# Between two stages: modulated rows by transposing back, residual rows made later, no elementwise work on POOL, accumulators summed by transfer

## The chip, the cores and the metric

The kernel runs on one NeuronCore of a Trainium2 chip. The metric is the device time of one execution in microseconds. The engines are PE (matrix multiply), DVE (VectorE), ACT (ScalarE), POOL (GpSimd) and SP, which here only issues transfers. Transfers issued by POOL are written out by software on that engine. PE reads SBUF and writes PSUM; DVE and ACT read both; POOL reads SBUF alone.

## What is computed

A trunk of two layers over 256 context rows and 512 latent rows of 1024 channels. Layer 0 mixes by a gated linear recurrence (called lru below), layer 1 by a delta-rule recurrence (rwkv). Each mixer is followed by a mixture of 64 experts, of which each row takes 8, and a shared expert. What lies between the stages is this:

```python
def _layer_norm(h, g, b):
    mu = jnp.mean(h, -1, keepdims=True); var = jnp.mean(jnp.square(h - mu), -1, keepdims=True)
    return (h - mu) * lax.rsqrt(var + LN_EPS) * g + b

def _modulate(h, shift, scale):
    return h * (1.0 + scale) + shift

for i in range(2):                       # m[0..5] are rows made from c by ada_w, for ctx and lat apart
    y = mixer_i(_modulate(h, m[0], m[1]))
    h = _layer_norm(ALPHA * h + m[2] * y, post_ln_g[i, 0], post_ln_b[i, 0])
    u = _modulate(h, m[3], m[4])
    y = moe_i(u)                         # router, 8 of 64 experts, shared expert
    h = _layer_norm(ALPHA * h + m[5] * y, post_ln_g[i, 1], post_ln_b[i, 1])
```

Layer 1 needs the latent rows alone behind its mixer, so there are six tiles of 128 rows in layer 0 and four in layer 1.

## The kernel before

The program runs eight stages in order: the lru mixer; the first output stage (rows out of the mixer, norm, modulation, routing); the first expert stage; the first transition (norm behind the experts, rows turned to channels for the next mixer); the rwkv mixer with its projections at the start; the second output stage; the second expert stage; and the end (norm behind the experts, rows out). Except for the loop over the experts, which is laid out by hand, a scheduler orders the instructions of each engine at build time from a simulation; on the chip each engine takes its own list in order, and semaphores hold it where something is not there yet.

**Output stages.** `outputs` (line 423) runs over the row tiles. For tile t it issues the product of the mixer's output with its last weights (`gemm`, two PSUM buffers of two banks) and steps a generator `res` (line 1934) that does the rest in pieces split by `yield`: load the old rows `hin`; norm (`post_ln`, line 395, in layer 0; in layer 1 the product holds all of it and `norm`, line 409, is called alone); turn the normed tile to channels by eight PE transposes into the PSUM tile `rt_px` (one buffer), evict it by eight ACT instructions with a scale and bias per channel to `rt_uT` (L1960), which holds the modulated rows as channels; make the same modulated rows in row form by two POOL instructions (L1961, L1962) for the store to `u_d`, from which the experts gather; make the residual rows, gain and bias applied, by two more (L1964, L1965) and store them to `hm_d`; then `route` (line 677). `post_ln` and `norm` run on DVE: mean and variance by `bn_stats` (L414), then an inverse square root in some dozen instructions on 128 single numbers (L314 to L326), and one ACT instruction that normalises (L421). `prepare` loads the rows of gains, biases and modulation, spread over 128 partitions (`mb`), and combines them on POOL and DVE (L1915 to L1918). Between the pieces, `Early` feeds in parts of the shared expert, whose weights are split into a high and a low part by ACT and by DVE or POOL (`ew`, L305 and L308). The routing of the last tile ends with `Mt`, which the sort of the experts waits for (L790).

**Behind the experts.** The experts add their rows into two accumulators in DRAM, turn about. `start` (line 1997) loads a tile of each, `tile_` (line 2005) adds the two on DVE (L2007), scales by m[5] on POOL (L405, in `post_ln`), adds the old rows on DVE (L406), norms, applies the gain on POOL (L2010) and the bias on DVE (L2011), and stores. In the first transition the six tiles go on into `rwkv` (line 1059), where each is turned to channels by eight PE transposes and evicted with scale and bias `mT` by ACT (L1136) and DVE (L1133) in turn, into `u`. The stored rows `h1_d` are read again at the second output stage.

Of the kernel before, what the change touches and what calls it, by code (L numbers as in the profile page):

```python
# [9 lines left out]
F32 = mybir.dt.float32  # L10
# [9 lines left out]
D = 1024  # L20
# [251 lines left out]
class Kern:  # L272
# [122 lines left out]
    def post_ln(self, wk, h, y, m2b, zn, z):  # L395
# [8 lines left out]
        else:  # L404
            nc.gpsimd.tensor_tensor(z, y, m2b, op=OP.mult)  # L405
# [17 lines left out]
    def outputs(self, n, gemm, res, early=None, last=None, read=None):  # L423
# [5 lines left out]
        for t in range(n + 1):  # L429
            if t < n:  # L430
# [3 lines left out]
                if t == n - 1 and early:  # L434
                    last()
                    early.begin()
                    feed()
            go(t - 1)
# [6 lines left out]
            go(t - 1)  # L445
            feed()
        if early:
            early.drain()
# [610 lines left out]
    def rwkv(self, first, done, prepare, res):  # L1059
# [5 lines left out]
        with ExitStack() as st:  # L1065
# [14 lines left out]
            for n, ap in (("mu", ins["rwkv_mu"][0].rearrange("c (k p) -> (c k) p", p=128)),  # L1080
# [4 lines left out]
                          ("rk", ins["rwkv_r_k"][0].rearrange("(k t) e -> k (t e)", t=2))):  # L1085
# [13 lines left out]
            with ExitStack() as s1:  # L1099
# [7 lines left out]


                zr = b1.tile([48, D], F32, name="zr")
                nc.gpsimd.memset(zr, 0.0)  # L1110
                nc.scalar.activation(indT.rearrange("h j p -> h (j p)"), zr, AF.Copy)
                nc.scalar.activation(rn, zr[:, :NTOK], AF.Copy)
# [13 lines left out]
                for t in range(NT):  # L1126
# [112 lines left out]
                for j in range(KD):  # L1239
# [4 lines left out]
                    nc.sync.dma_start(r_d[j * 128:(j + 1) * 128, :], kf[:, :NLAT])  # L1244

# [634 lines left out]
def trunk(tc, ins, out):  # L1880
# [3 lines left out]
    with ExitStack() as st:  # L1884
# [5 lines left out]
        h1_d = dp.tile([NTOK, D], F32, name="h1_d")  # L1890
        u_d = [dp.tile([n + 128, D], F32, name=f"u_d{i}") for i, n in enumerate((NTOK, NLAT))]
# [8 lines left out]
        def mixer_res(i):  # L1900
            P = {}

            def prepare(pool, psr):
                lg, lb = K.ln_params(pool, i, 0)
                P["ln"] = lg, lb
                S = (CTX, LAT) if i == 0 else (LAT,)
                for q, s in [(q, s) for s in S for q in (2, 3, 4)]:
                    P[q, s] = pool.tile([128, D], F32, name=f"mb{q}{s}")
                    if (q, s) != (2, LAT):
                        K.bcast_row(P[q, s], i, s, q)  # L1910
# [196 lines left out]
```

## Time and profile before

| | us |
|---|---|
| median of 3 runs | 3386.93 |
| lowest, highest | 3377.25, 3399.31 |
| the profiled execution | 3388.3 |
| its span, first to last instruction | 3386.4 |

The profile follows one execution. It has the busy time of each engine, the span in 40 slices, the instructions grouped by line with their mean duration and the idle time before them, the instructions in order of time, and the busy time of each engine in chosen stretches together with the clock granted to PE (1.00 is 2.4 GHz, 0.50 is 1.2 GHz). A duration on DVE or POOL holds also the time in which the instruction was held up once it had begun.

### The profile page before, as it was taken

The numbers are of one execution on the slowest core, as the hardware profiler recorded it, in microseconds if no ns is written. First come the engines' busy times: TensorE is split into PE (matmuls) and PEld (weight loads), VectorE is DVE, ScalarE is ACT, GpSimd is POOL, SyncE is SP. The second block draws the span as 40 slices with busy tenths as digits, with TensorE's granted clock in tenths as the row PEclk, the third lists the DMA queues.
The fourth block names the chain that finished last, engine by engine and source line by source line (L and its number), as shares of the span: only waits on it lengthen the run. The fifth ranks groups of instructions, "written<-read, shape, count | busy, mean of one in ns | idle before, by whom it ended". The sixth has DMA issues, their size and how long they took to land. (4 is left out here: it accounts for less than half of the span.)

```text
span 3386.4 us, 52288 instructions
## 1 busy us (share of the span) xinstructions
PE 2934.2 (87%) x17769; PEld 2051.6 (61%) x17769; DVE 2470.1 (73%) x4665; ACT 1967.2 (58%) x3771; POOL 1274.7 (38%) x1401
## 2 busy tenths in 40 slices
PE   7998758899999998298989899998976898899993
PEld 3665746666676664276757677676655665555551
DVE  3555878788878886867774677675466888789886
ACT  2765236677766776466655455553432766677772
POOL 0323543334334432422444445453453233334333
PEclk8998879999999999599985766678788999999996
DMA  6446349999999998333675765667545999999994
GB/s 219 120 138 197 136 182 273 300 330 330 336 296 319 329 319 283 130 92 118 148 192 145 190 178 143 180 176 194 159 151 185 327 316 332 326 355 352 347 337 152
DMA packets 331073, 789.94 MB, mean 233 GB/s; under 512 B 129320, under 2 KB 194136, under 8 KB 281264
## 3 DMA queue, kind: packets, MB, share of 16 engines
q1 hardware_dynamic: 278848, 676.74, 60.6%
q0 software_dynamic: 51952, 109.78, 13.4%
q8 instruction: 145, 2.38, 0.3%
q14 instruction: 128, 1.05, 0.1%
HBM read 649.90 MB, written 134.82 MB: 232 GB/s over the span
## 5 line engine op out<-in xcount | busy, mean ns | idle before, releaser
L95 PE MATMUL ph<-w1s,xs 128*128 128x512 f32 (+21 forms) x3216 | 806.4, 400 | 5.7 <-ACT xs L305 3.9
L1031 POOL DMA_INDIRECT acc_d<-yt,ix x150 | 316.7, 2112 | 933.6 <-ACT yt L141 338.9
L308 DVE TENSOR_TENSOR w1s<-w,w1s 128x1024 fp32r<-128x1024 f32 x516 | 609.2, 1222 | 63.6 <-ACT w1s L305 62.8
L95 PEld LDWEIGHTS ph<-w1s,xs 128*128 128x128 f32 (+21 forms) x3216 | 489.9, 156 | 246.5 <-DVE xs L308 10.8
L305 ACT ACTIVATE w1s<-w 128x1024 fp32r<-128x1024 f32 x516 | 516.9, 1057 | 3.9 <-DMA w<-in_moe_w_gu_dram 3.3
L95 PE MATMUL py<-w2s,hT 128*128 128x512 f32 (+22 forms) x1608 | 429.5, 416 | 50.4 <-DVE yt L138 30.3
L95 PEld LDWEIGHTS py<-w2s,hT 128*128 128x128 f32 (+22 forms) x1608 | 250.2, 163 | 174.7 <-issue 36.8
L305 ACT ACTIVATE xs<-px 128x512 fp32r<-128x512 f32 (+23 forms) x287 | 131.0, 456 | 361.0 <-DVE xs L308 238.5
L308 DVE TENSOR_TENSOR w2s<-w,w2s 128x1024 fp32r<-128x1024 f32 x258 | 303.7, 1218 | 16.2 <-ACT w2s L305 15.9
L305 ACT ACTIVATE w2s<-w 128x1024 fp32r<-128x1024 f32 x258 | 258.4, 1053 | 23.4 <-DMA w<-in_moe_w_down_dram 23.3
L308 DVE TENSOR_TENSOR xs<-px,xs 128x512 fp32r<-128x512 f32 (+23 forms) x287 | 146.4, 510 | 149.7 <-ACT xs L305 146.6
L929 POOL DMA_INDIRECT xg<-u_d,ix x150 | 209.0, 1393 | 86.0 <-issue 39.8
L141 ACT ACTIVATE yt<-py 128x512 f32<-128x512 f32 (+20 forms) x282 | 151.5, 593 | 45.5 <-PE py L95 30.0
L73 PE MATMUL px<-ident,xg 128*128 128x128 f32 (+25 forms) x1224 | 129.3, 249 | 30.6 <-DMA xg<-u_d,ix 30.6
L1680 POOL TENSOR_TENSOR SU<-SU,pC 64x128 f32<-64x128 f32 x176 | 86.3, 495 | 167.9 <-DVE SU L1700 140.8
L539 PE MATMUL in_ps<-uT,w_in 128*128 128x256 f32 (+1 forms) x768 | 144.2, 346 | 4.3 <-ACT w_in L305 2.3
L73 PEld LDWEIGHTS px<-ident,xg 128*128 128x128 f32 (+25 forms) x1224 | 110.8, 144 | 53.4 <-issue 45.1
L539 PEld LDWEIGHTS in_ps<-uT,w_in 128*128 128x128 f32 x768 | 119.5, 191 | 35.3 <-ACT w_in L305 7.4
L1179 PE MATMUL pt_ps<-xm,rw 128*128 128x256 f32 (+1 forms) x600 | 130.0, 372 | 11.9 <-ACT xm L305 6.5
L1525 PE MATMUL sc_ps<-X,uBK 64*128 64x128 f32 (+1 forms) x768 | 133.5, 367 | 2.0 <-POOL upt L1484 0.7
L1700 DVE TENSOR_TENSOR SU<-SU,pg 64x128 f32<-64x128 f32 x176 | 48.2, 276 | 116.3 <-PE pg L1698 102.1
L1179 PEld LDWEIGHTS pt_ps<-xm,rw 128*128 128x128 f32 x600 | 104.1, 196 | 41.1 <-issue 8.9
(455 smaller groups left out, 5762.6 us busy)
## 6 DMA issues: line engine op xcount, KB each, us to landing
w<-in_moe_w_gu_dram SPq DMA_DIRECT2D x256, 1024.0 KB
w<-in_moe_w_down_dram SPq DMA_DIRECT2D x128, 1024.0 KB
ada_w<-in_ada_w_dram SPq DMA_DIRECT2D x96, 512.0 KB
O<-op SPq DMA_DIRECT2D x32, 768.0 KB
op<-NN SPq DMA_DIRECT2D x48, 256.0 KB
op<-NN SPq DMA_DIRECT2D x32, 384.0 KB
SU<-v_d SPq DMA_DIRECT2D x48, 256.0 KB
acc_d<-zrow SPq DMA_DIRECT2D x17, 512.0 KB
```

The source lines that it names most:

```text
L73: self.nc.tensor.transpose(px[:, k, :C], x[:C, k * 128:(k + 1) * 128], self.K.ident[:C, :C])
L95: self.nc.tensor.matmul(out[:C], x[a][:, :C], w[b], start=(first and a + b == 0), stop=(last and a == 1))
L141: self.nc.scalar.activation(yt[:C, c * 512:(c + 1) * 512], py[:C, c, :], AF.Copy)
L305: nc.scalar.activation(hi, src, AF.Copy)
L308: (lo_eng or nc.vector).tensor_tensor(lo, src, hi.bitcast(F32), op=OP.subtract)
L539: nc.tensor.matmul(ps[:, s, :n], whl[a][:, k, :], uT[b][:, k, t0:t0 + n], start=(k == 0 and a == 0 and b == 0), stop=(k == KD - 1 and a == 1))
L929: nc.gpsimd.indirect_dma_start(out=x[:C], out_offset=None, in_=u_d, in_offset=bass.IndirectOffsetOnAxis(ap=IW[blk][0], axis=0))
L1031: nc.gpsimd.indirect_dma_start(out=acc_d[n % 2], out_offset=bass.IndirectOffsetOnAxis(ap=ix, axis=0), in_=yt[:C], in_offset=None, compute_ ...
L1179: nc.tensor.matmul(ps[:, s, :n], w[a][:, k, :], x[k][b][:, s0:s0 + n], start=(k == 0 and a == 0 and b == 0), stop=(k == KD - 1 and a == 1))
L1525: nc.tensor.matmul(sc[h][:, c, :nr, :], BK[r64(h), c].rearrange("p a t -> p (a t)"), X[r64(h), :, c, :], start=True, stop=True)
L1680: nc.gpsimd.tensor_tensor(SV[z, g2][r64(0), :, k2], S[r64(0), :, k], P[z, g]["pC"][:, k].to_broadcast([64, 2, 64]), op=OP.mult)
L1700: nc.vector.tensor_tensor(S, S, pg[:, 2], op=OP.add)
```

## The change

- `res`: the four POOL instructions are gone. A second set of eight ACT evictions of the same `rt_px`, with gain and bias per channel, makes `rt_hT`. A helper `back` turns a channel tile into rows again: eight PE transposes into a new `rt_px` and two ACT copies of 128x512. It is called for `rt_uT`, then the store to `u_d`, and for `rt_hT`, then the store to `hm_d`, each behind a `yield` of its own after `route`.
- `outputs` steps the generators once more per tile in two places, and once behind the loop.
- `prepare` keeps of the spread rows only m[2] in layer 0; the loads of the others and the twelve instructions that combine them (eight in layer 0, four in layer 1) are gone.
- `post_ln`: the product with m[5] moves from POOL to DVE.
- `start` loads one accumulator per tile; the other is added to it by a transfer from DRAM into SBUF, issued by POOL.
- `tile_`: the addition is gone. In layer 0 gain and bias are no longer applied; the normed rows go to `z1_d`. In layer 1 both are applied on DVE.
- `rwkv`: the gain and bias are folded into the scale and bias per channel (`cs`), and all eight evictions of a tile are on ACT. The rows of `h1_d` are made among the projections: four tiles of `z1_d` are loaded, multiplied on DVE, added to on POOL and stored.

```diff
@@ post_ln
-            nc.gpsimd.tensor_tensor(z, y, m2b, op=OP.mult)
+            nc.vector.tensor_tensor(z, y, m2b, op=OP.mult)
@@ outputs
+            go(t - 2)
             go(t - 1)
             feed()
             go(t)
...
             feed()
             go(t - 1)
+            go(t - 1)
             feed()
+        go(n - 1)
@@ rwkv
+                cs = b1.tile([128, 2, KD, 2], F32, name="cs")
...
-                        if k % 2:
-                            nc.vector.tensor_scalar(u[:, k, t * 128:(t + 1) * 128], ps[:, k, :], mT[:, 8 + k, s:s + 1],
-                                                    mT[:, k, s:s + 1], op0=OP.mult, op1=OP.add)
-                        else:
-                            nc.scalar.activation(u[:, k, t * 128:(t + 1) * 128], ps[:, k, :], AF.Identity,
-                                                 scale=mT[:, 8 + k, s:s + 1], bias=mT[:, k, s:s + 1])
+                        nc.scalar.activation(u[:, k, t * 128:(t + 1) * 128], ps[:, k, :], AF.Identity,
+                                             scale=cs[:, 0, k, s:s + 1], bias=cs[:, 1, k, s:s + 1])
...
+                for t in range(2, NT):
+                    hf = wk.tile([128, D], F32, name="hf", tag="gf")
+                    self.load(hf, z1_d[t * 128:(t + 1) * 128, :])
+                    nc.vector.tensor_tensor(hf, hf, hg[0], op=OP.mult)
+                    nc.gpsimd.tensor_tensor(hf, hf, hg[1], op=OP.add)
+                    nc.sync.dma_start(h1_d[t * 128:(t + 1) * 128, :], hf)
@@ res
-                nc.gpsimd.tensor_tensor(u, h, P[4, s], op=OP.mult)
-                nc.gpsimd.tensor_tensor(u, u, P[3, s], op=OP.add)
-                nc.sync.dma_start(u_d[i][t * 128:(t + 1) * 128, :], u)
-                nc.gpsimd.tensor_tensor(h, h, P["ln"][0], op=OP.mult)
-                nc.gpsimd.tensor_tensor(h, h, P["ln"][1], op=OP.add)
-                nc.gpsimd.dma_start(hm_d[i][t * 128:(t + 1) * 128, :], h)
+                hT = wk.tile([128, KD, 128], F32, name="rt_hT", bufs=1)
+                for k in range(KD):
+                    nc.scalar.activation(hT[:, k], px[:, k], AF.Identity, scale=x[:, 0, k:k + 1], bias=x[:, 1, k:k + 1])
+                def back(xT, y):
+                    px = psr.tile([128, KD, 128], F32, name="rt_px")
+                    for k in range(KD):
+                        nc.tensor.transpose(px[:, k, :], xT[:, k], K.ident)
+                    for k in range(0, KD, 4):
+                        nc.scalar.activation(y[:, k * 128:k * 128 + 512].rearrange("p (k d) -> p k d", k=4), px[:, k:k + 4, :], AF.Copy)
                 yield
                 K.route(t, uT, wk, psr)
+                yield
+                back(uT, u)
+                nc.sync.dma_start(u_d[i][t * 128:(t + 1) * 128, :], u)
+                yield
+                back(hT, h)
+                nc.gpsimd.dma_start(hm_d[i][t * 128:(t + 1) * 128, :], h)
@@ moe_res
-                    P["z", t] = pool.tile([128, D], F32, name="z", bufs=4)
-                    K.load(P["z", t], acc_d[i][1][t * 128:(t + 1) * 128, :])
+                    nc.gpsimd.dma_start(P["y", t], acc_d[i][1][t * 128:(t + 1) * 128, :], accum_op=OP.add)
...
-                nc.vector.tensor_tensor(yt, yt, P.pop(("z", t)), op=OP.add)
                 h = P["h", t]
                 K.post_ln(P["pool"], h, yt, P[5, stream(i, t)], h, yt)
-                nc.gpsimd.tensor_tensor(h, h, P["ln"][0], op=OP.mult)
-                nc.vector.tensor_tensor(h, h, P["ln"][1], op=OP.add)
                 if i == 0:
                     if t >= 2:
-                        nc.sync.dma_start(h1_d[t * 128:(t + 1) * 128, :], h)
+                        nc.sync.dma_start(z1_d[t * 128:(t + 1) * 128, :], h)
                 else:
+                    nc.vector.tensor_tensor(h, h, P["ln"][0], op=OP.mult)
+                    nc.vector.tensor_tensor(h, h, P["ln"][1], op=OP.add)
```

## Rows read from the trace of the kernel before

**Rows 1.** The page: busy us, share of the span and count of each engine.

```profile
PE 2934.2 (87%) x17769; PEld 2051.6 (61%) x17769; DVE 2470.1 (73%) x4665; ACT 1967.2 (58%) x3771; POOL 1274.7 (38%) x1401
```

**Rows 2.** Five stretches: length, busy PE, PEld, DVE, ACT, POOL; PE clock, DMA share, GB/s.

```profile
349.00:472.00 123.00, 84.77 (x482) 74.76 (x482) 114.68 (x291) 37.61 (x75) 76.63 (x37) 0.81 0.30 107
499.00:1344.00 845.00, 784.09 (x4125) 553.99 (x4125) 704.01 (x1062) 579.49 (x874) 298.77 (x188) 0.97 0.98 312
1353.00:1427.00 74.00, 14.89 (x59) 10.93 (x59) 62.62 (x134) 26.11 (x55) 32.31 (x30) 0.52 0.36 128
1427.00:1610.00 183.00, 169.62 (x767) 128.97 (x767) 126.83 (x200) 125.61 (x227) 41.71 (x26) 0.93 0.35 107
2497.00:2571.00 74.00, 46.88 (x198) 37.57 (x199) 62.02 (x170) 26.29 (x55) 50.23 (x24) 0.75 0.18 70
```

**Rows 3.** In order of time, first output stage, DVE and POOL: start, duration, engine, line.

```profile
372.93 2.20 DVE L322 SCALAR_TENSOR_TENSOR rs_t<-ln_rs,rs_x 128x1 f32<-128x1 f32 x1
382.15 0.22 DVE L322 SCALAR_TENSOR_TENSOR rs_t<-ln_rs,rs_x 128x1 f32<-128x1 f32 x1
...
372.69 2.42 POOL L1962 TENSOR_TENSOR um<-um,mb 128x1024 f32<-128x1024 f32 x1
```

**Rows 4.** Groups by line, first output stage: count, busy us, mean ns, idle before.

```profile
L322 DVE SCALAR_TENSOR_TENSOR rs_t<-ln_rs,rs_x 128x1 f32<-128x1 f32 x18 | 15.6, 875 | 0.2
...
L414 DVE BATCH_NORM_STATS2 ln_st<-hin 128x6 f32<-128x512 f32 x12 | 7.7, 679 | 0.0
```

**Rows 5.** In order of time: eight transposes, eight channel evictions, two row copies.

```profile
370.33 1.04 PE L1951 MATMUL rt_px<-ident,hin 128*128 128x128 f32 x8
371.41 2.90 ACT L1960 ACTIVATE rt_uT<-rt_px,mbc 128x128 f32<-128x128 f32 x8 [2.44 <-PE rt_px L1951]
481.89 1.09 ACT L141 ACTIVATE yt<-py 128x512 f32<-128x512 f32 x2 [4.36 <-PE py L95]
```

**Rows 6.** In order of time, first output stage: a product, the first norm and the end.

```profile
353.25 8.01 PE L650 MATMUL o_ps<-wo,yT 128*128 128x512 f32 x23 [11.94 <-DVE hin L403]
366.58 2.38 ACT L421 ACTIVATE hin<-hin,ln_nm,ln_rs 128x1024 f32<-128x1024 f32 x2 [43.24 <-DVE ln_nm L420]
471.52 0.26 PE L790 MATMUL cc<-ones_b,Mt 128*64 128x64 bf16 x1 [10.88 <-DVE Mt L709]
```

**Rows 7.** Groups by line, first transition.

```profile
L2007 DVE TENSOR_TENSOR late_w2s<-late_w2s,z 128x1024 f32<-128x1024 f32 x6 | 12.3, 2045 | 5.5 <-DMA z<-acc_d 5.5
L2011 DVE TENSOR_TENSOR late_w<-late_w,late_w 128x1024 f32<-128x1024 f32 x2 | 2.4, 1214 | 0.0
```

**Rows 8.** In order of time, first transition: first addition, next weights, next product.

```profile
1358.37 1.23 DVE L2007 TENSOR_TENSOR late_w2s<-late_w2s,z 128x1024 f32<-128x1024 f32 x1 [4.16 <-DMA z<-acc_d]
1417.44 0.43 SPq L299 DMA_DIRECT2D rw_f<-in_rwkv_w_in_dram  x1
1426.61 1.01 PE L1179 MATMUL pt_ps<-xm,rw 128*128 128x256 f32 x2 [5.19 <-ACT xm L305]
```

**Rows 9.** In order of time, second output stage; last line a POOL group of it.

```profile
2501.40 2.30 ACT L421 ACTIVATE hin<-ro_ps,ln_nm,ln_rs 128x1024 f32<-128x1024 f32 x2 [6.59 <-DVE ln_nm L420]
2548.73 9.19 DVE L692 TENSOR_TENSOR rt_gs<-rt_g 128x8 f32<-128x8 f32 x1
2571.64 0.28 PE L790 MATMUL cc<-ones_b,Mt 128*64 128x64 bf16 x3
...
L308 POOL TENSOR_TENSOR ew<-ew,ew 128x1024 fp32r<-128x1024 f32 x6 | 14.1, 2364 | 6.0 <-ACT ew L305 6.0
```

**Rows 10.** In order of time, the end: the first addition and the last bias.

```profile
3340.10 1.23 DVE L2007 TENSOR_TENSOR late_w2s<-late_w2s,z 128x1024 f32<-128x1024 f32 x1 [13.73 <-DMA z<-acc_d]
...
3378.39 1.22 DVE L2011 TENSOR_TENSOR late_w1s<-late_w1s,late_w 128x1024 f32<-128x1024 f32 x1 [2.23 <-POOL late_w1s L2010]
```

**Rows 11.** Transfers issued by POOL: form, count, size, median us to landing.

```profile
hm_d<-hin POOLq DMA_DIRECT2D x10, 512.0 KB, 3.0
acc_d<-yt POOLq DMA_DIRECT2D x10, 512.0 KB, 11.3
```

More of the change, by code (lines that the diff above doesn't have):

```diff
@@ L1056, in moe, with rwkv @@
                     nc.gpsimd.dma_start(acc_d[0][t * 128:(t + 1) * 128, :], yt, accum_op=OP.add)
-    def rwkv(self, first, done, prepare, res):
+    def rwkv(self, first, done, prepare, res, z1_d, h1_d):
         nc, ins, tc = self.nc, self.ins, self.tc
@@ L1084, in rwkv @@
                           ("ka", ins["rwkv_k_a"][0].rearrange("(k p) -> k p", p=128)),
-                          ("rk", ins["rwkv_r_k"][0].rearrange("(k t) e -> k (t e)", t=2))):
+                          ("rk", ins["rwkv_r_k"][0].rearrange("(k t) e -> k (t e)", t=2)),
+                          ("lg", ins["post_ln_g"][0, 1].rearrange("(k p) -> k p", p=128)),
+                          ("lb", ins["post_ln_b"][0, 1].rearrange("(k p) -> k p", p=128))):
                 self.load(prow[o:o + ap.shape[0]], ap)
@@ L1106, in rwkv @@
                 nc.vector.tensor_copy(pc, pps)
[L1109 to L1112, printed above, removed]
+                cs = b1.tile([128, 2, KD, 2], F32, name="cs")
+                bk = lambda n: pc[:, PO[n]:PO[n] + KD, None].to_broadcast([128, KD, 2])
+                nc.vector.tensor_tensor(cs[:, 0], mT[:, 8:16], bk("lg"), op=OP.mult)
+                nc.vector.tensor_tensor(cs[:, 1], mT[:, 8:16], bk("lb"), op=OP.mult)
+                nc.vector.tensor_tensor(cs[:, 1], cs[:, 1], mT[:, 0:8], op=OP.add)
+                zr = b1.tile([128, D], F32, name="zr")
+                nc.gpsimd.memset(zr[:48], 0.0)
+                nc.scalar.activation(indT.rearrange("h j p -> h (j p)"), zr[:48], AF.Copy)
+                nc.scalar.activation(rn, zr[:48, :NTOK], AF.Copy)
                 ind = b1.tile([128, KD, 16], F32, name="ind")
@@ L1244, in rwkv @@
                     nc.sync.dma_start(r_d[j * 128:(j + 1) * 128, :], kf[:, :NLAT])
+                hg = [zr, wk.tile([128, D], F32, name="hg", bufs=1)]
+                for x, n in zip(hg, ("post_ln_g", "post_ln_b")):
+                    self.load(x, ins[n][0, 1:2, :].to_broadcast([128, D]))
+                for t in range(2, NT):
[4 more added lines that the diff above has]
+                    nc.sync.dma_start(h1_d[t * 128:(t + 1) * 128, :], hf)
                 x = mix(5, NCTX)
@@ L1890, in trunk @@
         h1_d = dp.tile([NTOK, D], F32, name="h1_d")
+        z1_d = dp.tile([NTOK, D], F32, name="z1_d")
         u_d = [dp.tile([n + 128, D], F32, name=f"u_d{i}") for i, n in enumerate((NTOK, NLAT))]
@@ L1903, in prepare @@
             def prepare(pool, psr):
-                lg, lb = K.ln_params(pool, i, 0)
-                P["ln"] = lg, lb
                 S = (CTX, LAT) if i == 0 else (LAT,)
[L1907 to L1910, printed above, removed]
-                t = P[2, LAT]
-                for s in S:
-                    b, g = P[3, s], P[4, s]
-                    nc.gpsimd.tensor_scalar(g, g, 1.0, 1.0, op0=OP.mult, op1=OP.add)
-                    nc.vector.tensor_tensor(t, g, lb, op=OP.mult)
-                    nc.vector.tensor_tensor(b, b, t, op=OP.add)
-                    nc.gpsimd.tensor_tensor(g, g, lg, op=OP.mult)
-                    if s == LAT and i == 0:
-                        K.bcast_row(t, i, s, 2)
+                for s in S:
+                    if i == 0:
+                        P[2, s] = pool.tile([128, D], F32, name=f"mb{s}")
+                        K.bcast_row(P[2, s], i, s, 2)
                     r = pool.tile([4 * KD, 128], F32, name=f"mbr{s}")
@@ L1986, in late @@
                 P["ln"] = []
-                for x in ("post_ln_g", "post_ln_b"):
+                for x in ("post_ln_g", "post_ln_b")[:2 * i]:
                     P["ln"].append(row())
@@ L2054, in trunk @@
         P = {}
-        K.rwkv(first, done, begin, res)
+        K.rwkv(first, done, begin, res, z1_d, h1_d)
         with P["rs"]:
```

2 lines of the change are left out of this document (added).

## The prediction

> **What bounds the kernel now.** I read the page's line of engines first, then the busy time in stretches cut at the borders of the stages, then in each stretch the groups by line and the instructions in order of time. PE is busy for 87% of the span [rows 1], so the reader should ask where it is not. In the experts it is, 784 of 845 us [rows 2]. In the stretches between stages it is not: 85 of 123 us, 15 of 74, 47 of 74, and little in the 40 us of the end, where DVE is busy for 115, 63 and 62 us [rows 2]. So the change can reach some 310 us of the span, and there DVE sets the pace.
>
> Much of DVE's time is no work. An instruction on 128 single numbers takes 0.22 us alone and 2.20 us while POOL reads rows of 128x1024 for 2.42 us [rows 3]. L322 in the first output stage loses 15.6 − 18×0.22 = 11.6 us so, and a norm has a dozen like it; `bn_stats`, which reads one tensor, keeps 0.68 us [rows 4]. One DVE instruction of the routing of the second output stage takes 9.19 us [rows 9].
>
> The Trainium skill, page "SBUF — State Buffer", section "Who interferes with whom", says that a DVE instruction with two SBUF inputs and a POOL instruction that reads SBUF exclude one another, and that one with a single input is left alone outside its fast modes. The trace agrees (2.20 against 0.22, and `bn_stats` at 0.68). By this rule the POOL rows that the change leaves go on stalling DVE: rival B.
>
> **First output stage.** Removed: 24 POOL row instructions, the eight that combine rows, and the DVE stalls behind them. Added per tile: 16 transposes, 2×1.04 us on PE [rows 5], and on ACT eight more evictions of channels (2.90 us) and four 128x512 copies (two take 1.09 us): 2.90 + 2×1.09 = 5.1 us [rows 5]. Over six tiles that is 12.5 us on PE and 30.5 us on ACT. Two ways to the new length:
> - By sums: PE then works 84.8 + 12.5 = 97.3 us [rows 2]. With DVE's stalls gone and ACT at 37.6 + 30.5 = 68, PE is the largest. From the first product at 353.2 that ends at 450.5, where `Mt` stands now at 471.5 [rows 6]: 21 us.
> - By the ring: `rt_px` has one buffer, now used three times per tile: 1.04 + 2.90 + 2.90 + 2×(1.04 + 1.09) = 11.1 us, and I estimate 1.6 us of handing over between engines: 12.7. The first norm stands at 366.6 [rows 6]; four DVE combinations of 1.21 (the duration of such an instruction, L2011 [rows 7]) go ahead of it, so 361. The sixth tile reaches its transposes at 361 + 5×12.7 = 424.5; transposes, evictions and a routing of some 20 short DVE instructions, 11 us together, bring `Mt` to 435.5: 36 us if nothing holds the ring.
>
> Between the two stands what a tile waits in PE's list behind other work, w per tile: gain = 36 − 5w. The sums give 21, which is w = 3. I take 21; bounds 5 (w about 6, the ACT rival) and 36.
>
> **Second output stage.** The same for four tiles. The first norm moves from 2501.4 [rows 9] to about 2498, the combinations being gone; the fourth tile's transposes stand at 2498 + 3×12.7 = 2536, `Mt` at 2547 instead of 2571.6 [rows 9]: 24 − 3w, 15 at w = 3; bounds 5 and 24. Here POOL keeps the six splits of `ew`, 14.1 us [rows 9].
>
> **First transition.** Now DVE waits for two loads, adds (1.23 at 1358.4 [rows 8]), waits for POOL's product, adds the old rows, norms, waits for POOL's gain, adds the bias: 62.6 us busy in 74 [rows 2]. The addition averages 2.05 us, against 1.21 undisturbed [rows 7]. In the new one DVE does per tile the product with m[5] (1.21), the old rows (1.21), `bn_stats` (2×0.68) and a dozen short ones, about 2.0: 5.8 us, 34.7 for six. The transfer that adds the second accumulator must start when the first load has landed, at about 1357.4. No row shows an addition from DRAM into SBUF. The nearest are a POOL transfer of 512 KB, 3.0 us to landing, and one that adds 512 KB into DRAM, 11.3 [rows 11]. It is nearer to the first, as it writes SBUF and waits behind no scatter; I take 4.6, so DVE starts at 1362; bounds 1360.6 and 1369. Then 1362 + 34.7 = 1396.7, normalising on ACT 1.2, and the store and the next weights' issue (1417.4 now [rows 8]) at about 1398; the first product comes 9.2 later, as now: 1407.2 instead of 1426.6 [rows 8]. Gain 19; bounds 12 and 24. All eight evictions of a tile on ACT cost 2.90 us, beside DVE's 5.8: hidden; without that cover 1.5 us per tile.
>
> The Trainium skill, page "DMA: Bandwidth & Descriptors", section "Anatomy of one DMA — SWDGE (gpsimd) path", has a fit by which 512 KB take 3.2 us, an estimate of that page; by it DVE starts 1.2 us earlier and the sum is 1 us less. No row here shows such a transfer.
>
> **The end.** It starts 3.6 us later for the transfer (3340.1 + 3.6 [rows 10]); DVE then takes per tile 5.8 + 2×1.21 = 8.2, for four 32.9, to 3376.6, and 1.5 of normalising and handing over: 3378.1, instead of 3379.6 (3378.39 + 1.22 [rows 10]). Gain 1; bounds −5 and 6. Three more engines' hand-overs are gone, but DVE takes their work.
>
> **Residual rows among the projections.** The stretch of 183 us behind the transition has PE at 169.6 and DVE at 126.8 [rows 2]. Added are ten transfers of 512 KB on SP's queue (two of gain and bias, four loads, four stores), 4×1.21 = 4.9 us of DVE and 4×2.42 = 9.7 of POOL. Cover is there: DVE has 56 us free, DMA is at a share of 0.35. What can be late is the weight loads queued on SP behind a load of `hf`, which waits for a free buffer, and behind a store, which waits for POOL. Cost 2; bounds 0 and 10 (POOL's 9.7 wholly as DVE's stall).
>
> Ten row loads of 512 KB in the mixers are gone as well (four of gain and bias, six of modulation); they lie beside matmuls, and I count nothing. If they were not covered they would be a gain of a few us. The experts behind are the same instructions and move as a whole.
>
> **Sum.** 21 + 15 + 19 + 1 − 2 = 54. The profiled execution took 3388.3 us, 1.4 above the median, within the runs' spread; 3388.3 − 54 = 3334. The bounds of the terms, not all at one end, give the forecast its own range, 3304 to 3353.
>
> **Rivals.**
> - *A. The ring and ACT eat the output stages.* `rt_px` with three uses waits on ACT, which serves the mixer's evictions and the `ew` splits too. For: ACT nearly doubles there, 37.6 to 68 us. Against: 68 of 100 is not full. With w = 6.3 the stages give 36 − 31 = 5 and 24 − 19 = 5: 5 + 5 + 19 + 1 − 2 = 28, 3360. Chance 0.13.
> - *B. The POOL work that stays keeps DVE stalled.* Three splits of `ew` that I count in the first stage (3×2.36), six in the second (14.1, 2.36 each [rows 9]) and 9.7 in the projections are 31 us; wholly on the chain they leave 23: 3365. For: the 9.19 us [rows 9]. Against: most short DVE instructions fall between them. Chance 0.06.
> - *C. The adding transfers are slow.* 11.3 us each, one behind the other, on POOL's queue: DVE waits for each. Six end at 1357.4 + 68 = 1425, and the product stands at about 1441: −15; four at the end, −14. 21 + 15 − 15 − 14 − 2 = 5: 3383. For: the only adding transfer in the trace [rows 11]. Against: that one goes by list into DRAM while the experts fill the queues. Chance 0.07.
> - *D. The other side: PE's fixed order.* The transposes back stand in PE's list. If they wait there for ACT, the mixer's next product (8.0 us a run of 23 [rows 6]) waits behind them, and the next tile's transposes behind that product: w = 8 + 2×2.9 = 14. Then the stages give 36 − 70 = −34 and 24 − 42 = −18, the sum is −34 − 18 + 19 + 1 − 2 = −34: 3422. It decides from the w at which 60 − 8w + 18 is nothing, 9.8. For: PE now stands idle 10 us and more behind DVE in that list [rows 6]. Against: the generators are stepped so that a product lies between each part and the next. Chance 0.10.
>
> **How the numbers follow.** The forecast keeps 0.64: the stalls are measured, and the removed POOL work cannot return. A measurement of this kernel can tell about 1%, 34 us, from no change, so faster means below 3353, slower above 3421. Faster: the forecast, 0.64, and slivers of A and B, 0.02. Slower: D, 0.10. Same: the rest, 0.24. The range goes from 3302, the forecast's lower bound, to 3368, which takes in A and B and leaves out C, D and the forecast's far ends, 2 in 10.
>
> **What would show it.** Right: L322 at about 0.25 us in the output stages (0.88 before); `Mt` near 450 and, within its stage, 15 us sooner in the second; the first projection's product 19 us sooner after the experts' end; uses of `rt_px` 15 to 16 us per tile; the adding transfer landing in 3 to 6 us. Wrong: idle PE ended by ACT on `rt_px` (A, D); DVE instructions of 2 us beside POOL's `ew` or `hf` (B); DVE waiting for a transfer into the accumulators' tiles at L406 or the product with m[5] (C); or an experts' stage whose length moves, which I have as fixed.

## The result, and the profile after

The changed kernel took 3413.86 us (median of 20 runs, 3384.67 to 3433.64), the kernel before 3389.56 in the same measurements. The ratio is 1.0075, 95% interval 1.0052 to 1.0098: 24 us longer, where 54 us less was forecast. The profiled execution of after took 3411.85 us, its span 3410.0, so both profiles lie near their medians and can be set against each other.

The first line of the page says that the work moved as planned: DVE fell from 2470 to 2351 us, POOL from 1275 to 1135 [rows 1].

```profile
PE 2990.5 (88%) x17929; PEld 2086.7 (61%) x17929; DVE 2350.9 (69%) x4640; ACT 2023.0 (59%) x3915; POOL 1134.9 (33%) x1349
```

I cut both spans at instructions that both kernels have: the last `Mt` of the first output stage, the first product of the first experts, their last first-layer product, the first `pt_ps` and the first `l_ps` of the projections, the last `pt_ps`, the first `kk_ps` (the delta-rule scan of the second mixer begins), the first `ro_ps` (read-out), the first transposes of `hin` in the second output stage, its `Mt`, the experts' first product, the end. Each length is the difference of two start times in the order-of-time view. A minus in the last two columns means time lost.

| stretch | before | after | forecast gain | measured gain |
|---|---|---|---|---|
| start to last `Mt` (first output stage in it) | 471.5 | 466.9 | 21 | 4.6 |
| experts' end to first `pt_ps` (transition) | 93.6 | 82.1 | 19 | 11.5 |
| first `pt_ps` to first `l_ps` (first projections) | 22.9 | 36.8 | −2 | −13.9 |
| scan | 794.2 | 815.3 | 0 | −21.1 |
| first `ro_ps` to first `hin` transposes | 106.1 | 113.6 | 0 | −7.5 |
| first `hin` transposes to `Mt` (second output stage) | 69.0 | 70.7 | 15 | −1.7 |
| that `Mt` to the experts' first product | 36.7 | 40.1 | 0 | −3.4 |
| experts and end | 778.0 | 771.6 | 1 | 6.4 |
| the rest together | 1014.4 | 1012.9 | 0 | 1.5 |
| span | 3386.4 | 3410.0 | 54 | −23.6 |

So there are three findings: the gains where the change was made are 20.8 us (4.6 + 11.5 − 1.7 + 6.4) and not 56; the residual rows took 13.9 us and not 2; and 29 us were lost in the scan and the read-out behind it (21.1 + 7.5), of whose instructions the change takes out only the four that combine rows for the second output stage.

**The output stages.** The DVE stalls are gone: L322 takes 213 ns where it took 875 [rows 4], and DVE is busy for 60 us of the stage where it was 115 [rows 2]. The stage's busy time by halves (columns as in [rows 2]) and what PE waited for, after:

```profile
350.00:410.00 60.00, 59.53 (x399) 54.76 (x400) 28.64 (x130) 27.97 (x64) 1.16 (x2) 0.96 0.21 77
410.00:467.00 57.00, 37.15 (x170) 30.44 (x168) 31.32 (x145) 38.66 (x83) 8.73 (x6) 0.71 0.30 111
```

```profile
L322 DVE SCALAR_TENSOR_TENSOR rs_t<-ln_rs,rs_x 128x1 f32<-128x1 f32 x18 | 3.7, 213 | 0.0
```

```profile
PE rt_px L1977 <- ACT rt_hT L1971: 5.5, 3, 2.4
PE rt_px L1958 <- ACT hin L1979: 3.5, 3, 1.2
PE rt_pr L685 <- ACT rt_uT L1967: 3.5, 3, 2.4
```

PE works 96.7 us, as forecast (97.3), but in 117 us. In the first 60 it is full: the mixer's last product is through at 409 (424 before). Then three of the six tiles are still to go, none of the mixer's products is left to lie between their steps (only some of the shared expert's are), and PE waits for ACT at eight of the ten uses of `rt_px`. All waits for ACT in these 57 us come to 19.1 of the 19.9 in which PE is idle. The granted clock is at 0.71 there, between its two levels of 1.2 and 2.4 GHz, after 0.96 while PE was full.

**The second output stage** in order of time: the first use of `rt_px` of each of its four tiles, and `Mt`. A tile takes 16.6 to 21.5 us, where it took 10.3 to 16.5 before; the tail behind the last fell from 28.7 to 11.9.

```profile
2527.66 1.97 PE L1958 MATMUL rt_px<-ident,hin 128*128 128x128 f32 x8 [7.09 <-ACT hin L421]
2548.35 1.09 PE L1958 MATMUL rt_px<-ident,hin 128*128 128x128 f32 x8 [1.18 <-ACT hin L1979]
2569.86 1.03 PE L1958 MATMUL rt_px<-ident,hin 128*128 128x128 f32 x8
2586.45 1.09 PE L1958 MATMUL rt_px<-ident,hin 128*128 128x128 f32 x8 [0.71 <-ACT hin L1979]
2598.36 0.37 PE L793 MATMUL cc<-ones_b,Mt 128*64 128x64 bf16 x3
```

**The transition and the first projections**, after, in order of time: POOL issues the first adding transfer, DVE can begin, DVE ends, the first product. Then groups by line of the stretch behind it (1411 to 1448), and the transfer's group.

```profile
1349.80 0.98 POOL L2021 DMA_DIRECT2D late_w2s<-acc_d  x1
1359.20 1.22 DVE L405 TENSOR_TENSOR late_w2s<-late_w2s,late_w 128x1024 f32<-128x1024 f32 x1 [11.38 <-DMA late_w2s<-acc_d]
...
1394.38 0.21 DVE L420 TENSOR_SCALAR ln_nm<-ln_mv,ln_rs 128x1 f32<-128x1 f32 x1
...
1410.82 1.01 PE L1186 MATMUL pt_ps<-xm,rw 128*128 128x256 f32 x2 [8.15 <-ACT xm L305]
```

```profile
L1162 DVE SCALAR_TENSOR_TENSOR xmf<-u,rcol,xmf 128x255 f32<-128x255 f32 (+1 forms) x16 | 20.3, 1314 | 2.1 <-ACT xmf L1156 2.0
...
L1260 POOL TENSOR_TENSOR hf<-hf,hg 128x1024 f32<-128x1024 f32 x4 | 10.3, 2580 | 3.0 <-issue 1.8 <-DVE hf L1259 1.2
```

```profile
late_w2s<-acc_d POOLq DMA_DIRECT2D x10, 512.0 KB, 11.2
```

DVE's part of the transition takes 35.4 us (1359.2 to 1394.6), near the forecast (34.7). It began 9.4 us after the issue of the transfer, and from its end to the first product 16 us went by, where I had 10.5. Then the residual rows came at once: all four run in the first 30 us of the projections, where DVE and PE are tight, and not in the 56 us that DVE has free later. L1162 took 1314 ns an instruction while POOL read the rows. The same line of before, from its first `pt_ps` to its first `l_ps`, took 740:

```profile
L1155 DVE SCALAR_TENSOR_TENSOR xmf<-u,rcol,xmf 128x255 f32<-128x255 f32 (+1 forms) x16 | 11.2, 740 | 3.2 <-ACT xmf L1149 3.0
```

**The scan and the read-out**, from the first `kk_ps` to the first transposes of `hin` (columns as in [rows 2]): before, after, and n2, which is before with an edit that does nothing (below):

```profile
1602.35:2502.66 900.31, 818.70 (x7043) 610.91 (x7042) 571.29 (x1490) 457.90 (x1390) 416.75 (x814) 0.74 0.65 174
1598.75:2527.66 928.91, 838.33 (x7043) 621.21 (x7042) 556.50 (x1493) 459.23 (x1395) 412.79 (x812) 0.73 0.63 167
1603.15:2515.38 912.23, 819.80 (x7042) 610.67 (x7041) 570.23 (x1495) 457.14 (x1395) 411.65 (x814) 0.74 0.65 173
```

Between these two points PE has the same instructions in every version. The first `ro_ps` does not divide them in the same way: in after, 32 instructions that stand ahead of it in before stand behind it. So the scan and the read-out of the table belong together, 28.6 us. DVE, ACT and POOL are busy for as long, within 2 us, or less. PE is busy for 20 us more at a granted clock of 0.73 for 0.74, and it is idle for 9 us more (90.6 for 81.6). What differs is the order: the scheduler, which orders from a simulation, gave PE a list that differs from that of before in over a hundred places between the projections and the second output stage, and the other engines' lists with it.

### The profile page after: what moved, and what is told of

It is laid out like the page before. It is cut to its first block, busy times and chain, and to the rows that moved or that the text cites. A ratio compares the mean times of both kernels' runs of the same rounds, so it can differ in the third digit from the quotient of the medians.

```text
span 3410.0 us, 52638 instructions
## 1 busy us (share of the span) xinstructions
PE 2990.5 (88%) x17929; PEld 2086.7 (61%) x17929; DVE 2350.9 (69%) x4640; ACT 2023.0 (59%) x3915; POOL 1134.9 (33%) x1349
## 5 line engine op out<-in xcount | busy, mean ns | idle before, releaser
L95 PEld LDWEIGHTS ph<-w1s,xs 128*128 128x128 f32 (+21 forms) x3216 | 490.9, 157 | 246.3 <-DVE xs L308 11.2
L95 PE MATMUL py<-w2s,hT 128*128 128x512 f32 (+22 forms) x1608 | 434.6, 421 | 49.3 <-DVE yt L138 31.4
L305 ACT ACTIVATE w2s<-w 128x1024 fp32r<-128x1024 f32 x258 | 258.4, 1053 | 18.7 <-DMA w<-in_moe_w_down_dram 18.5
```

The source lines that it names most:

```text
L95: self.nc.tensor.matmul(out[:C], x[a][:, :C], w[b], start=(first and a + b == 0), stop=(last and a == 1))
L305: nc.scalar.activation(hi, src, AF.Copy)
```

## The experiments

All medians are from executions beside the kernel before on the same chip, whose own medians there were 3388.2 to 3394.6; so differences of two runs are taken between their distances from it, the third column. Lengths are from one profile each, cut as above. "Scan to `hin`" is the scan with the read-out. The last column is the time of the profiled execution: the lowest of its kernel in x1_outputs and n3, the highest in y3 and c1, so these lengths don't stand for the median.

| run | median | less before's, beside it | ratio, 95% | experts' end to `pt_ps` | `pt_ps` to `l_ps` | scan | scan to `hin` | second stage | profiled |
|---|---|---|---|---|---|---|---|---|---|
| before | 3389.6 |  |  | 93.6 | 22.9 | 794.2 | 900.3 | 69.0 | 3388.3 |
| after | 3413.9 | +24.3 | 1.0075 (1.0052 to 1.0098) | 82.1 | 36.8 | 815.3 | 928.9 | 70.7 | 3411.9 |
| x1_outputs | 3412.4 | +24.0 | 1.0066 (1.0040 to 1.0092) | 93.4 | 22.7 | 795.6 | 904.2 | 70.5 | 3388.3 |
| x1_again (one execution) | 3425.7 | +31.1 |  | 94.9 | 22.7 | 823.5 | 931.7 | 70.9 | 3425.7 |
| x2_between | 3379.2 | −9.2 | 0.9967 (0.9938 to 0.9996) | 83.7 | 36.7 | 786.2 | 894.2 | 69.4 | 3375.4 |
| x3_rows_dve | 3397.8 | +9.4 | 1.0018 (0.9999 to 1.0036) | 82.9 | 32.5 | 797.8 | 911.5 | 71.4 | 3388.9 |
| y3_rows_in_transition | 3403.1 | +12.7 | 1.0027 (1.0002 to 1.0051) | 86.6 | 23.4 | 818.0 | 931.0 | 69.7 | 3411.9 |
| n2_neutral | 3398.8 | +10.4 | 1.0024 (1.0000 to 1.0048) | 92.8 | 22.6 | 795.8 | 912.2 | 68.6 | 3399.0 |
| n3_three_memsets | 3401.6 | +13.4 | 1.0033 (1.0011 to 1.0054) | 92.4 | 22.6 | 784.8 | 902.1 | 68.7 | 3382.6 |
| y1_outputs_neutral | 3397.3 | +6.9 | 1.0005 (0.9976 to 1.0034) | 93.6 | 22.7 | 788.6 | 903.8 | 70.3 | 3398.7 |
| a1_after_neutral | 3416.3 | +25.9 | 1.0075 (1.0050 to 1.0101) | 83.3 | 37.4 | 815.0 | 937.0 | 70.9 | 3425.2 |
| y2_hT_on_dve | 3410.0 | +19.6 | 1.0059 (1.0032 to 1.0087) | 82.2 | 37.1 | 820.4 | 936.9 | 63.8 | 3411.6 |
| y4_two_banks | 3388.2 | −6.4 | 0.9991 (0.9965 to 1.0017) | 83.1 | 36.2 | 782.4 | 897.6 | 61.4 | 3376.0 |
| c1_banks_and_rows | 3398.1 | +9.9 | 1.0031 (1.0003 to 1.0059) | 86.3 | 22.7 | 823.4 | 937.2 | 66.8 | 3414.5 |
| c2_same_neutral | 3397.8 | +9.6 | 1.0004 (0.9975 to 1.0033) | 86.2 | 23.3 | 819.4 | 931.6 | 66.6 | 3400.7 |
| c3_banks_rows_dve | 3389.8 | +1.6 | 1.0003 (0.9980 to 1.0027) | 82.5 | 31.0 | 823.4 | 936.1 | 62.6 | 3401.0 |
| s0_before | 3716.3 | +321.7 | 1.0942 (1.0901 to 1.0982) | 95.7 | 25.5 | 1083.2 | 1177.7 | 83.5 | 3715.9 |
| s0_after | 3651.4 | +256.8 | 1.0759 (1.0720 to 1.0798) | 75.8 | 32.3 | 1089.3 | 1185.9 | 53.4 | 3656.4 |

**The change in two halves.** x1 has the edits of `res`, `outputs` and of what `prepare` keeps; x2 all others.

```diff
 x1: before, and from the change
+                back(uT, u)
+                back(hT, h)
+            go(t - 2)
 x2: before, and from the change
+                    nc.gpsimd.dma_start(P["y", t], acc_d[i][1][t * 128:(t + 1) * 128, :], accum_op=OP.add)
+            nc.vector.tensor_tensor(z, y, m2b, op=OP.mult)
+                    nc.gpsimd.tensor_tensor(hf, hf, hg[1], op=OP.add)
```

> The kernel before with the parts for the two output stages alone (transposing back, no POOL rows, fewer combined rows). Theory 1 (the ring of the one PSUM tile and ACT eat the gain where it arises): first output stage 3 to 7 us shorter than before, second output stage 0 to 5 us longer, first transition and projections as before. Theory 2 (the delta-rule scan of the second mixer changes length because the build-time scheduler lays its order out anew, whatever was edited ahead of it): the scan, 795 us before and 816 after from the first L1445 to the first ro_ps, comes out anywhere from 780 to 825. Rival (the scan is lengthened by the work that the parts between the stages put into it): the scan stays at 795 within 5, total 3382 to 3392.

> The kernel before with the other parts alone (accumulators summed by transfer, product on DVE, residual rows among the projections); the output stages are those of before. Theory 1: transition about 12 to 16 us shorter, the first 20 us of the projections 10 to 14 us longer, the end 3 to 6 shorter, so 5 to 10 us in all without the scan. Theory 2: scan anywhere from 780 to 825. Rival: scan near 816, total about 3400.

x1 took 3412 in the median, nearly all that the whole change costs, though its last `Mt` of the first stage comes 2.2 us sooner and its second stage is 1.5 longer. In its profile the scan had the length of before; but that profile is of its fastest execution (3388). x1_again is one more execution of the same program:

> The part for the output stages alone once more, for one more profile, since the first fell on its fastest execution (3388, median 3412). Theory 2: scan 805 to 822 (795.6 in the fastest execution) with the other stages as they were; if the 24 us lie elsewhere, scan 793 to 800 again.

This execution took 3425.7, and its scan 823.5, just above the forecast 805 to 822: one program, one list, and in the scan 28 us between two executions. The two scans:

```profile
1598.60:2394.20 795.60, 732.26 (x6486) 548.22 (x6485) 514.79 (x1342) 427.46 (x1312) 374.66 (x743) 0.74 0.65 172
```

```profile
1601.80:2425.30 823.50, 755.36 (x6486) 564.67 (x6485) 517.91 (x1344) 428.19 (x1312) 374.56 (x743) 0.71 0.64 166
```

The other engines work as long in both, within 4 us; PE works 23 us longer at a lower granted clock. So the scan has most of what lies between these two executions (28 of 37 us), and it goes with the clock: of the 20 executions of after, the shortest (3384.67) had a mean clock of 0.881 over the span, the longest (3433.64) 0.865. A kernel's median then depends on the clock that it mostly gets there, and one profile of the scan doesn't give it.

x2 took 3379.2. Its stages give what theory 1 says: transition −9.9, projections +13.8, end −4.4 (from the last product of the experts). The scan, 786.2 in that profile of a 3375 us execution, is within the range of theory 2 and not the 816 of the rival. It is the one version whose whole interval lies below the kernel before, by 0.04 to 0.62%.

**Edits that do nothing.** Eight memsets of a tile that nobody reads, ahead of the projections (n2; in n3 three):

```diff
                 om = b1.tile([128, 6 * KD], F32, name="om")
+                dz = b1.tile([128, 256], F32, name="dz")
+                for _ in range(8):
+                    nc.vector.memset(dz, 0.0)
```

> The kernel before with eight short DVE memsets of an unused tile added at the start of the projections, some 1 to 2 us of DVE by themselves. The order of the scan's instructions on PE is laid out anew by it. Theory 2: the scan differs from 795 by more than 8 us, up or down, and the total with it by up to 25 us. Rival: scan 795 within 5, total 3386 to 3392.

> The kernel before with three memsets in place of eight. PE's order is that of the neutral run with eight (which took 3399 in the median, before 3388 to 3391), not that of before. Theory 2: what counts is the order, so 3394 to 3404 again. Rival (the memsets' own time): 3389 to 3394.

n2 came out 10 us above before (its interval begins at 1.0000), n3 13. PE's list is the same in n2 and n3 and another than in before. With three memsets as long as with eight, it isn't their own time. My number for n2's scan (over 8 us from 795) was missed: its profile has 795.8. But the new list has 52 instructions more behind the first `ro_ps`, and up to the first `hin` it takes 912.2 us where before takes 900.3. So the loss is in this profile, of an execution at the median, as 11 us more of idle PE at the same granted clock, 0.74. n3's profile, of its lowest execution, has 902.1. The same memsets were put into the part for the output stages and into after:

> The part for the output stages alone with the same eight short DVE memsets ahead of the projections as in the neutral run. They lay the order of the scan out anew; the output stages' instructions are those of the part alone, which took 3412 in the median. Theory 2 (what the scan takes is a matter of the order it happens to get, at a granted clock that goes with it): the median moves by 8 us or more from 3412, likeliest downwards, 3380 to 3404, with the stages outside the scan within 2 us of the part alone. Rival (the parts for the output stages lengthen the scan by what they do): 3412 to 3416.

> The kernel after with the same eight memsets; here the order of PE, ACT, POOL and SP stays as it is, so this measures what the eight memsets themselves take. Theory 2: nothing that can be measured, 3411 to 3418, against 3413.9. Rival (the 10 us of the neutral run are the memsets' own): 3422 to 3426.

In y1 they change PE's list, and the distance from before falls from 24 us to 7; the two intervals don't meet. In after they leave the lists of PE, ACT, POOL and SP as they are, and the median moves little: 26 us against 24, the scan 815.0 against 815.3 (the read-out, in an execution of 3425, 121.9 against 113.6). So where the list stays, the median stays (after and a1, n2 and n3). Where it changes, the median moves: by 10 and 13 us up in n2 and n3, which are one list, and by 17 down in y1. One more case, c2 against c1 below, shows no such move.

The windows from the first `kk_ps` to the first `hin` tell two parts of this apart. PE's idle time there differs by 5 us at most between executions of one list: 92.4 and 97.0 us in n2 and n3, 90.6 and 94.9 in after and a1, 90.6 and 93.4 in the two executions of x1. Its busy time goes with the execution and its clock: 813.6 and 838.3 in those two. Before has 81.6 us of idle time in its one profile, less than each of the other lists that the simulation made (89.4 to 99.3). So its own list may be a lucky one, which any edit gives up; that is argued, not shown.

**The order held.** Built by priority alone, without the simulation, both kernels have one PE list through the scan but for its beginning and end:

```diff
-    with tile.TileContext(nc, schedule_with_timeline_sim=True) as tc:
+    with tile.TileContext(nc, schedule_with_timeline_sim=False) as tc:
```

> The kernel before, built without the timeline simulation in the scheduler, so that instructions are ordered by priority alone. Slower or faster in itself; it serves as the partner of the next run: in this pair the order of PE through the scan is the same but for its first tenth and its last products. No number expected but a scan length to compare.

> The kernel after, built in the same way. Theory 2 (the scan lengthened by its new order, not by the change): with the order held, the scan is within 6 us of its partner's, and the pair differs by what the stages themselves give, the total 0 to 15 us shorter than the partner's. Rival (the change lengthens the scan by transfers, buffers or heat that it leaves behind): scan 15 to 25 us longer than the partner's here too, total 5 to 25 longer.

Both are much slower for it, but against one another the change takes 65 us away: 3716.3 to 3651.4. By stretches of the profiles: first stage 19.8 gained (forecast 21), transition 19.9 (19), second stage 30.1 (15), residual rows 6.8 lost (2), scan 6.1 lost (0), read-out 2.1 lost (0), experts and end 5.6 gained (1). In the scan PE has equally many instructions in both. The scan's 6.1 is just beyond the 6 that I had set for theory 2 and far from the rival's 15 to 25; the total went far past my 0 to 15. The first output stage of s0_after, from where the mixer's last product ends:

```profile
446.00:482.00 36.00, 24.70 (x125) 19.03 (x124) 23.97 (x82) 28.60 (x59) 8.24 (x5) 0.83 0.38 138
```

Here the mixer's products lie between the tiles' steps for longer, and 36 us follow the last of them, not 57 as in after. From the first `o_ps` to the last `Mt` it is 139.4 us here (342.6 to 482.0) and 152.9 in after (314.1 to 466.9), with the same instructions.

**The residual rows.** In x3 the addition is on DVE; in y3, which is x2 otherwise, the rows are made in the transition:

```diff
 x3: after
-                    nc.gpsimd.tensor_tensor(hf, hf, hg[1], op=OP.add)
+                    nc.vector.tensor_tensor(hf, hf, hg[1], op=OP.add)
 y3: x2, without the loop over hf
-                        nc.sync.dma_start(z1_d[t * 128:(t + 1) * 128, :], h)
+                        nc.vector.tensor_tensor(yt, h, P["ln"][0], op=OP.mult)
+                        nc.vector.tensor_tensor(yt, yt, P["ln"][1], op=OP.add)
+                        nc.sync.dma_start(h1_d[t * 128:(t + 1) * 128, :], yt)
```

> The kernel after with the addition of the residual rows among the projections on DVE in place of POOL. If POOL's reads are what stalls DVE there, the first products of the projections (first pt_ps to first l_ps, 37 us after, 23 before) take 27 to 31 us and L1162 falls from up to 2 us to about 0.6 to 0.9. If it is DVE's own added work and the queue of the loads, they take 36 to 42. The total moves by that and by what the scan does (theory 2: anywhere from 780 to 825; rival: 816 as after).

> The parts between the stages alone, but the residual rows are made in the first transition, on DVE, into the tile that the norm leaves free, and not among the projections. If their place beside POOL's reads among the first projections is what costs: first pt_ps to first l_ps back from 36.7 to 22 to 25 us, the transition 2 to 9 longer than the 83.7 of the part alone, net gain 5 to 12. If it is their DVE work and loads wherever they are: net gain under 3.

x3: 32.5 us from `pt_ps` to `l_ps`, between the two forecasts. L1162 fell from 1314 to 837 ns, so POOL's reads had stalled it; but POOL's own splits there, 2.88 us each in after, now take 4.15:

```profile
L308 POOL TENSOR_TENSOR xm<-xmf,xm 128x768 fp32r<-128x768 f32 x4 | 16.6, 4146 | 60.4 <-ACT xm L305 60.4
L1162 DVE SCALAR_TENSOR_TENSOR xmf<-u,rcol,xmf 128x255 f32<-128x255 f32 (+1 forms) x16 | 12.7, 837 | 3.8 <-ACT xmf L1156 3.7
```

So moving the addition from POOL to DVE gave back some 4 of the 14 us, net of DVE's own longer work; the rest is the rows' being there at all. y3 shows that: 23.4 us, as before the change, and 2.9 more in the transition, a net 10.4 us in these stretches, within the forecast. It stands 22 us above x2 all the same, with a scan of 818.0 in the profile of its slowest execution.

**The chain of `rt_px`.** y2 evicts `rt_hT` on DVE; y4 does so with each engine in the other half of the tile:

```diff
 y2: after
-                    nc.scalar.activation(hT[:, k], px[:, k], AF.Identity, scale=x[:, 0, k:k + 1], bias=x[:, 1, k:k + 1])
+                    nc.vector.tensor_scalar(hT[:, k], px[:, k], x[:, 0, k:k + 1], x[:, 1, k:k + 1], op0=OP.mult, op1=OP.add)
 y4: after
+                for a, b in ((0, 4), (4, 0)):
+                    for k in range(a, a + 4):
+                        nc.scalar.activation(uT[:, k], px[:, k], AF.Identity, scale=c[:, 0, k:k + 1], bias=c[:, 1, k:k + 1])
+                    for k in range(b, b + 4):
+                        nc.vector.tensor_scalar(hT[:, k], px[:, k], x[:, 0, k:k + 1], x[:, 1, k:k + 1], op0=OP.mult, op1=OP.add)
```

> The kernel after with the second set of eight evictions of a tile (rt_hT) on DVE in place of ACT. Theory 1 (one PSUM tile used three times, waiting for ACT each time, sets the pace of the output stages, 18.7 us per tile in the first and 19.6 in the second): the two sets run beside one another, 2 to 2.9 us less per tile, so the first stage ends 8 to 14 us sooner (Mt at 453 to 459, 466.9 after) and from the first to the last hin transposes of the second takes 50 to 54 us (58.8 after). Rival (the transposes back wait in PE's list behind other products and for the routing): under 4 us in either.

> The kernel after with rt_hT evicted on DVE, each engine in the half of the PSUM tile where the other is not, ACT first half first, DVE second half first; in the earlier run DVE began each set only when ACT had ended its own. Theory 1 (the one PSUM tile's chain sets the pace): 2.4 to 2.9 us less per tile where the chain is tight, that is the last three tiles of the first stage and all four of the second: Mt at 457 to 462 (466.9 after), first to last hin transposes of the second stage 48 to 52 us (58.8 after). Rival (PE's list): under 3 us in the first.

The first stage didn't get shorter: last `Mt` at 466.5 and 468.9 (after 466.9), where theory 1 had 453 to 459 and 457 to 462. The second got shorter by 6.9 and 9.3 us, and from its first to its last transposes of `hin` took 52.3 and 49.3, as theory 1 had it (50 to 54, 48 to 52; after 58.8). But neither run tests the theory as meant, since the engines did not work side by side. In a tile of y2's second stage ACT's set began at 2538.32 and took 2.89 us, and DVE began at 2541.24, as it ended. In y4 it was the same half by half:

```profile
456.73 1.51 ACT L1967 ACTIVATE rt_uT<-rt_px,mbc 128x128 f32<-128x128 f32 x4 [1.18 <-PE rt_px L1958]
...
458.27 1.37 DVE L1969 TENSOR_SCALAR rt_hT<-rt_px,mbx 128x128 f32<-128x128 f32 x4 [1.81 <-ACT rt_uT L1967]
```

The Trainium skill, page "PSUM — Partial Sum Buffer", section "PSUM bank collisions raise a hardware error", has it that two engines may not touch one bank at once. The trace agrees that they took turns in y2; in y4 they took turns in the two halves too, and no run here shows them at work on one tile together. y4 as a whole stands 31 us below after, of which its two output stages give 7; its profile, of an execution 12 us below its median, has 31 us less from the first `kk_ps` to the first `hin`.

**The parts put together.** c1 is y4 with y3's rows, c2 the same with the eight memsets, c3 is y4 with x3's addition on DVE:

```diff
 c1: y4, and
+                        nc.vector.tensor_tensor(yt, yt, P["ln"][1], op=OP.add)
 c2: c1, and
+                for _ in range(8):
+                    nc.vector.memset(dz, 0.0)
 c3: y4, and
+                    nc.vector.tensor_tensor(hf, hf, hg[1], op=OP.add)
```

> The run with two banks, and the residual rows made in the first transition as in the earlier run. By the stages alone 8 to 12 us less than the run with two banks (3388): 3376 to 3380. Theory 2: the scan gets a new order, and the total comes out between 3355 and 3400; from the kernel after the part between pt_ps and l_ps falls from 36.8 to about 23 us.

> The run before this one with the eight neutral memsets; PE's order in the scan differs from it. Theory 2: its median differs by 8 us or more from that run's, either way, with the stages outside the scan within 3 us of one another. Rival: within 4 us.

> The run with two banks, and the addition of the residual rows among the projections on DVE. By the stages alone 4 to 5 us less than the run with two banks: 3383 to 3385. Theory 2: between 3360 and 3410 by the order that the scan gets.

c1 has the projections back (22.7), but it stands 16 us above y4 and not 8 to 12 below; c3 stands 8 above. c2's list differs from c1's; the medians are 0.3 us apart, the ratios 1.0031 and 1.0004 with intervals that overlap. My theory 2 named 8 us or more there: not borne out. A new list can move the time; it need not.

## Why the forecast was wrong

- **What bounds the stretches** was right: DVE's stalls beside POOL's reads. L322 fell to 213 ns (I named 0.25 us), and with the scan's order held (s0) the change gained 59 us between the two profiles, where the sum said 54. That the total fits is in part luck: the second stage gained twice its term, and 15 us were lost where I had 2.
- **The sum of PE's work, "that ends at 450.5"**, is the step that failed in the first stage. PE's work was sized well (97.3 forecast, 96.7 measured), but I took PE as full throughout and the order of its list as given. In after the list puts the mixer's products early; then three tiles stand alone, 57 us with PE busy for 37: the missing 20 us, of which 19 are waits for ACT. With its other order s0_after needs 13.5 us less from the first product to `Mt` for the same instructions. Rival A, which I gave 0.13, has the size (5 us). Its cause, that ACT is in the way, shows in the waits; y2 and y4, which take a set off ACT, shortened the second stage and not the first, and the two engines took turns, so for the first stage it stays open.
- **The second stage, "15 at w = 3"**: the tail gained 16.8, but the four tiles lost 18.5 before it; by the forecast's own formula, 24 − 3w, the 1.7 lost are w = 8.6. Ordered by priority alone (s0) it gained 30.1.
- **The transition, 19**: DVE's 34.7 us was right to 0.7. Two terms were mis-sized: the adding transfer took 9.4 us to DVE's start, where I had 4.6 (rival C's size for one, 11.3, was nearer; but the six overlapped, so its sum of 68 us was wrong); and 16 us and not 10.5 lay between DVE's end and the first product. The transfer was also issued 3.3 us sooner behind the experts than I had it, so of the 7.5 us that are missing the way to the product has 5.7.
- **The end, 1**, gained 5.3 us from the experts' last product on (56.8 to 51.5), inside its bounds.
- **"Cover is there: DVE has 56 us free"** was the mean over 183 us. The scheduler put all the rows into the first 30 us, where nothing is free: 13.9 us and not 2, more than my bound of 10. Of this, the stall of DVE beside POOL (the mechanism of rival B) was worth about 4 us net by x3. The Trainium skill, page "SBUF — State Buffer", section "Who interferes with whom", has it that a DVE instruction with two SBUF inputs contends with a POOL instruction that reads SBUF. L1162 reads two SBUF tensors, and the trace agrees with 1314 ns beside POOL's additions and 837 without them (x3).
- **"The experts behind are the same instructions and move as a whole"** held for the experts (826.5 and 826.1). I had tacitly extended it to the scan, and put the scan at nothing without a reason. There it fails: 29 us in the scan and the read-out, the step that turned the sign, since the span without them would be 5 us shorter than before. No rival of mine had this place. D's 3422 lies near the 3414 by luck: it had 52 us lost in the output stages, which together gained 2.9.
- **Two slips in the text, of no weight:** 3.2 us in place of 4.6 start DVE 1.4 us earlier, not 1.2; and the forecast's lower end stands once as 3304 and once as 3302.

What is shown for the scan: x1, whose edits lie outside it but for the four combining instructions, has nearly the whole loss. A neutral edit that changes the lists moved the median by +10 and +13 us on before (one list, two runs) and by −17 on x1; one that changes them (c2) gave no clear move, and one that keeps them (a1) none at all (1.0075 both). With the order held the scan differs by 6 us and the read-out by 2. What stays open: why one order leaves PE idle for longer or gets a lower granted clock than another, and which engine's list it is, since they change together. The largest shift by a neutral edit is 17 us, so that much of the 29 is shown to be of this kind, and the rest is argued. One profile can't settle it, as two executions of x1 differ by 28 in the scan.

## What to carry to other kernels

Where a scheduler orders the instructions from a simulation, an edit is never local: make neutral edits as well, take the spread of their medians as the least that a change must exceed, and judge the change with the order held as well (here both kernels were 7 to 9% slower in that order, so it is a second view and no replacement). Free time of an engine, averaged over a stretch, covers nothing by itself; say at which moment the new work runs. And when a stall is removed, ask what lies between the steps that are left: here PE ran out of the mixer's products 57 us before the end of the stage. Cut stretches at points between which each engine has the same instructions; the first `ro_ps` was no such point.

## What the runs showed of the hardware

- A transfer that adds 512 KB from DRAM to tiles in SBUF took 11.2 us to landing (median of ten), as one that adds into DRAM did before (11.3 [rows 11]; 8.3 in after), and about four times the plain store (3.0).
- POOL's instructions take longer beside DVE's, as DVE's do beside POOL's: its split of 128x768 in the first projections took 2.18 us before, 2.88 beside four rows on DVE and POOL, and 4.15 when DVE did both operations on the rows.
- The same program's scan took 795.6 and 823.5 us in two executions, at granted clocks of 0.74 and 0.71, with the other engines' busy time within 4 us.
